# A hybrid decoder trunk on eight cores, rebuilt: transposed layouts, sample columns in the prompt blocks, chunk-dense state-space matmuls, stored tables and a list-scheduled instruction order

## The chip, the cores and the metric

The kernel runs on all eight cores of one Trainium2 chip, as two dies of four cores (0 to 3 and 4 to 7). Each core has its own prompt of 2048 positions and 16 of the 128 sample rows; the cores exchange nothing. The metric is the device time of the slowest core in microseconds (us). Rearranging arrays on the host, before and after the launch, is not in it.

A program on all eight cores has a second, slower state in some executions, in which the cores of one die, or of both, show a lower granted TensorE clock: in a run of the kernel before that took 5631.45 us, cores 4 to 7 took 5607 to 5630 us at a mean clock of 0.796 to 0.800, and cores 0 to 3 took 5072 to 5088 us at 0.908 to 0.919. Only executions in the fast state are compared here. Engine names are those of the profile: PE is the matmul engine, DVE is VectorE, ACT is ScalarE, POOL is GpSimd, SP is SyncE. A name such as L643 is a line of the kernel in question, so the same code can have another number in another version.

## The reference, cut to what matters

Four layers work on x of width 1024. A layer has a short convolution branch and a diagonal complex state-space branch, which are gated and merged, and then a feed-forward block. The same trunk runs over the prompt without a starting state, and over the sample rows, one position each, with a given state.

```python
def _layer(x, conv_buf, h0_re, h0_im, ...):
    h = _rmsnorm(x, norm1_g)
    z = h @ w_in                       # 1024 -> 4096: zb, zc, zv, zu, ga, gs
    conv_out, new_buf = _conv_causal(zc * zv, conv_buf, conv_w, conv_b)   # width 3
    ya = zb * conv_out
    ys, hr, hi = _s5(zu, h0_re, h0_im, lam_re, lam_im, log_dt, b_re, b_im, c_re, c_im, d_skip)
    gy = jax.nn.gelu(ys, approximate=False)
    ys = gy * jax.nn.sigmoid(gy @ w_glu + b_glu)
    m = jax.nn.sigmoid(ga) * (ya @ w_branch[:512]) + jax.nn.sigmoid(gs) * (ys @ w_branch[512:])
    x = x + m @ w_out
    h2 = _rmsnorm(x, norm2_g)
    gate, up = jnp.split(h2 @ w_gate_up, [2816], axis=-1)
    return x + (jax.nn.silu(gate) * up) @ w_down, new_buf, hr, hi

def _s5(u, ...):      # 32 groups of 16 channels, each with 64 complex states
    # state_t = abar * state_{t-1} + bbar u_t ;  y_t = Re(c . state_t) + d * u_t
```

## The kernel before: the parts that matter

Prompt positions go through in two halves of 1024, all four layers for one half and then for the other. Half 0 also carries the 16 sample rows, as a block of its own:

```python
def blocks(half):
    bl = [(0, 512, "p"), (512, 512, "p")]
    if half == 0:
        bl.append((1024, NS, "s"))          # NS = 16 columns
    return bl
```

The state-space recurrence is cut into chunks of T = 8 positions. Within a chunk everything is a matmul against tables (WBF, KF, CAF) that are powers of the state matrix times B and C. Between chunks VectorE rotates, scans, and rotates back. The matmuls use tiles of 32 rows or columns of the array and strided reads of the activations:

```python
for j in range(T):                      # part_a: within the chunk
    for tau in range(j + 1):
        for rg in range(4):
            mm(PSUM[b][32*rg:32*rg+32, j:512:T], KF[buf][:, tau, 32*rg:32*rg+32],
               R[32 rows..., UT + f, c0 + j - tau:c0 + 512:T], ...)      # 64 columns each
...
for j in range(T):                      # part_d: from the incoming state
    for rg in range(4):
        for ri in range(2):
            mm(PSUM[b][32*rg:32*rg+32, j:512:T], CAF[buf][:, ri, j+1, rg, :],
               HBF[:, ri, 4*f+rg, kb:kb+64], ...)
...
if f + 2 < 4:
    ssm_prep_ck(l, f + 2, f % 2)        # tables of quarter f + 2, built in line by VectorE
```

The tables of a layer are built for half 0 and again for half 1. The order of instructions on each engine is the order in which the program emits them. Weights come straight from their arrays with a casting DMA, 256 columns by 1024 rows a unit, into a ring of slots.

Of the kernel before, what the change touches and what calls it, by code (L numbers as in the profile page):

```python
# [12 lines left out]
D = 1024  # L13
# [5 lines left out]
T = 8  # L19
# [3 lines left out]
DBG = {"layers": DEPTH, "phases": None, "halves": 2}  # L23

class Op:
    __slots__ = ("eng", "fn", "deps", "needed", "val", "sem")

class Sched:
    ENGS = ("pe", "act", "dve", "pool", "sp")

    def __init__(self):
        self.prog = {e: [] for e in self.ENGS}
        self.last_w = {}
        self.readers = {}
        self.last_dma = {}

    def op(self, eng, fn, reads=(), writes=(), deps=(), dma_sem=None, mode=None):
        d = list(deps)
        forced = None
        if eng == "pe" and dma_sem is None:  # L40
            lp = getattr(self, "last_pe", None)
            if lp is not None and mode != self.last_pe_mode:
                forced = lp
        for k in reads:
            w = self.last_w.get(k)
            if w is not None:
                d.append(w)
        for k in writes:
            w = self.last_w.get(k)
            if w is not None:  # L50
                d.append(w)
            d.extend(self.readers.get(k, {}).values())
        if dma_sem is not None and dma_sem in self.last_dma:
            d.append(self.last_dma[dma_sem])
        o = Op()
        o.eng = eng
        o.fn = fn
        o.needed = False
        o.val = None
        o.sem = dma_sem  # L60
        dd = []
        seen = set()
        for x in d:
            if id(x) in seen:
                continue
            seen.add(id(x))
            if x.sem is None and x.eng == "pe" and eng == "pe" and dma_sem is None:
                continue
            x.needed = True
            dd.append(x)  # L70
        if forced is not None and id(forced) not in seen:
            forced.needed = True
            dd.append(forced)
        o.deps = dd
        if eng == "pe" and dma_sem is None:
            self.last_pe = o
            self.last_pe_mode = mode
        if dma_sem is not None:
            o.needed = True
            self.last_dma[dma_sem] = o  # L80
        rk = dma_sem if dma_sem is not None else eng
        for k in reads:
            self.readers.setdefault(k, {})[rk] = o
        for k in writes:
            self.last_w[k] = o
            self.readers[k] = {}
        self.prog[eng].append(o)
        return o

    def finalize(self):  # L90
        cnt = {e: 0 for e in self.ENGS}
        dcnt = {}
        for e in self.ENGS:
            for o in self.prog[e]:
                if o.sem is not None:
                    dcnt[o.sem] = dcnt.get(o.sem, 0) + 16
                    o.val = dcnt[o.sem]
                elif o.needed:
                    cnt[e] += 1
                    o.val = cnt[e]  # L100

    def runner(self, e, sems, dsems):
        def body(eng):
            waited = {}
            for o in self.prog[e]:
                for x in o.deps:
                    if x.sem is not None:
                        key = ("d", x.sem)
                        sh = dsems[x.sem]
                    else:  # L110
                        key = ("e", x.eng)
                        sh = sems[x.eng]
                    if waited.get(key, 0) >= x.val:
                        continue
                    waited[key] = x.val
                    eng.wait_ge(sh, x.val)
                ins = o.fn(eng)
                if o.sem is not None:
                    ins.then_inc(dsems[o.sem], 16)
                elif o.needed:  # L120
                    ins.then_inc(sems[e], 1)
        return body

def build():
# [8 lines left out]
    xp = din("xp", [SEQ, D])  # L133
    xs = din("xs", [NS, D])
    sconv_in = din("sconv", [DEPTH, NS, 2, CW])
    sre_in = din("sre", [DEPTH, NS, 2048])
    sim_in = din("sim", [DEPTH, NS, 2048])
    norm1_g = din("norm1_g", [DEPTH, D])
    w_in = din("w_in", [DEPTH, D, 4096])
    conv_w = din("conv_w", [DEPTH, 3, CW])  # L140
    conv_b = din("conv_b", [DEPTH, CW])
    lam_re = din("ssm_lam_re", [DEPTH, 32, 64])
    lam_im = din("ssm_lam_im", [DEPTH, 32, 64])
    log_dt = din("ssm_log_dt", [DEPTH, 32])
    b_re = din("ssm_b_re", [DEPTH, 32, 64, 16])
    b_im = din("ssm_b_im", [DEPTH, 32, 64, 16])
    c_re = din("ssm_c_re", [DEPTH, 32, 16, 64])
    c_im = din("ssm_c_im", [DEPTH, 32, 16, 64])
    ssm_d = din("ssm_d", [DEPTH, CW])
    w_glu = din("w_glu", [DEPTH, CW, CW])  # L150
    b_glu = din("b_glu", [DEPTH, CW])
    w_branch = din("w_branch", [DEPTH, D, D])
    w_out = din("w_out", [DEPTH, D, D])
    norm2_g = din("norm2_g", [DEPTH, D])
    w_gate_up = din("w_gate_up", [DEPTH, D, 2 * DFF])
    w_down = din("w_down", [DEPTH, DFF, D])
    final_g = din("final_g", [1, D])

    yp = dout("yp", [SEQ, D])
    ysm = dout("ysm", [NS, D])  # L160
    pconv_o = dout("pconv", [DEPTH, 2, CW])
    pre_o = dout("pre", [DEPTH, 16, 128])
    pim_o = dout("pim", [DEPTH, 16, 128])
    sconv_o = dout("sconv_o", [DEPTH, NS, 2, CW])
    sre_o = dout("sre_o", [DEPTH, NS, 2048])
    sim_o = dout("sim_o", [DEPTH, NS, 2048])
# [6 lines left out]
    NSLOT = 5  # L173
# [3 lines left out]
    RING = sb("RING", [128, NSLOT, 2048], BF16)  # L177
    NSCR = 8
    SCR = sb("SCR", [128, NSCR, 512])
    NSCB = 5  # L180
    SCB = sb("SCB", [128, NSCB, 512], BF16)
    GS = sb("GS", [128, 2, 16, 128])
    HBF = sb("HBF", [128, 2, 16, 129], BF16)
    TW = sb("TW", [128, 2, 16, 128])
    R8T = sb("R8T", [128, 16])
    TP = sb("TP", [128, 160])
    HC = sb("HC", [128, DEPTH, 2, 16])
    CONVST = sb("CONVST", [128, DEPTH, 2, 4])
    PT = sb("PT", [128, 256])
    LAMT = sb("LAMT", [128, 2, 64])  # L190
    LDT = sb("LDT", [128, 64])
# [3 lines left out]
    MASK2 = sb("MASK2", [128, 2])  # L195
    MASK4 = sb("MASK4", [128, 4])
    MASKC = sb("MASKC", [128, 128])
    MV = sb("MV", [128, 9, 16])
    PWR = sb("PWR", [128, 2, 9, 16])
    BXF = sb("BXF", [128, 2, 16, 32])  # L200
    BXB = sb("BXB", [128, 2, 16, 32], BF16)
    CXF = sb("CXF", [128, 2, 4, 128])
    WBF = [sb(f"WBF{i}", [128, 8, 2, 128], BF16) for i in range(2)]
    CAF = [sb(f"CAF{i}", [128, 2, 9, 4, 32], BF16) for i in range(2)]
    KF = [sb(f"KF{i}", [128, 8, 128], BF16) for i in range(2)]
    SST = sb("SST", [128, 2, 16, NS])
    SSTB = sb("SSTB", [128, 2, 16, NS], BF16)
    SNEW = sb("SNEW", [128, 2, 16, NS])
    SCV = sb("SCV", [128, 2, 4, NS])
    CINS = sb("CINS", [128, 4, NS])  # L210
    PSUM = [es.enter_context(nc.psum_tensor(f"ps{i}", [128, 512], F32)) for i in range(8)]
    NLD = 4
    sems = {e: es.enter_context(nc.semaphore(f"s_{e}")) for e in Sched.ENGS}
    dsem_names = [f"w{i}" for i in range(NSLOT)] + [f"ld{i}" for i in range(NLD)] + [f"st{i}" for i in range(4)]
    dsems = {k: es.enter_context(nc.semaphore(f"d_{k}")) for k in dsem_names}

    S = Sched()
    PHN = {"p": "init"}
    st = {"bank": 0, "scr": 0, "scb": 0, "ld": 0, "st": 0}

    def bank():
        b = st["bank"]
        st["bank"] = (b + 1) % 8
        return b

    def scr(n=1):
        if st.get("ffn"):
            if st.get("in_pf"):
                i = st.get("scr_pf", 0)
                if i + n > 6:  # L230
                    i = 0
                st["scr_pf"] = (i + n) % 6
                return i
            assert n == 1
            i = st.get("scr_ffn", 6)
            st["scr_ffn"] = 13 - i
            return i
        i = st["scr"]
        if i + n > NSCR:
            i = 0  # L240
        st["scr"] = (i + n) % NSCR
        return i

    def scb():
        i = st["scb"]
        st["scb"] = (i + 1) % NSCB
        return i

    def ldsem():
        i = st["ld"]  # L250
        st["ld"] = (i + 1) % NLD
        return f"ld{i}"
# [1079 lines left out]
```

## Time and profile before

The kernel's recorded runs were 5085.59, 5161.33, 5350.16 and 5457.22 us; the fast state is the low end of these. The profiled execution was fast: 5078.3 us, all cores between 5063 and 5078 us.

| reading | value | view |
|---|---|---|
| PE busy | 4300.6 us, 85% | first part of the page |
| DVE busy | 2603.9 us, 51% | first part of the page |
| 512-column matmuls in a dense stretch | 280 in 60.0 us, 214 ns each | windows |
| full-array matmuls of 512 columns (projections and norms) | 9728 + 5120 + 288 | groups by shape |
| matmuls altogether | 38,212 | first part of the page |

First the page of the kernel before: the span, the busy times, the weights' DMA queue and the chain that ended last.

```profile
span 5078.3 us, 99036 instructions; the slowest of 8 cores (5063.4 to 5078.3 us)
...
PE 4300.6 (85%) x38212; PEld 2288.2 (45%) x38212; DVE 2603.9 (51%) x4750; ACT 1031.0 (20%) x1985; POOL 434.5 (9%) x526
...
q0 software_dynamic: 479104, 243.30, 37.8%
...
PE 73%; DVE 15%; issue 6%; DMA 4%; ACT 3%; DVEq 0%; ACTq 0%; POOL 0%; SPq 0%; POOLq 0%
```

The engine that bounds the kernel is PE, but a quarter of the chain is something else. The windows view shows where. Its columns are the stretch in us, its length, the busy time (and number of instructions) of PE, weight load, DVE, ACT and POOL, the granted clock, the DMA share and GB/s. The first line is a state-space stage of half 1, the second a feed-forward stretch.

```profile
4620.00:4680.00 60.00, 25.78 (x905) 23.59 (x909) 40.41 (x59) 4.50 (x6) 0.00 (x0) 0.70 0.01 2
4920.00:4980.00 60.00, 60.00 (x280) 27.20 (x278) 13.43 (x20) 7.16 (x12) 7.95 (x10) 1.00 0.67 84
```

In the dense stretch, 280 matmuls fill the 60 us exactly, at a granted clock of 1.00. In the state-space stage, 905 tiny matmuls keep PE busy for 26 us, and the mean granted clock is 0.70; by the waits of this window PE waits 20 us for VectorE and 17 us for ScalarE. The view of waits names what PE waits for in such stages: CAF is a table, HBF the incoming state.

```profile
PE ps L760 <- DVE CAF L746: 140.1, 18, 10.3
PE ps L288 <- ACT HBF L993: 129.7, 16, 11.6
```

The sample rows cost separate matmuls. This is the timeline of PE (start, length, what, how many).

```profile
486.20 0.55 PE L288 MATMUL ps<-H,RING 128*128 128x16 bf16 x16
486.61 0.35 PE L288 MATMUL ps<-R,RING 128*128 128x16 bf16 x8
486.81 0.38 PE L288 MATMUL ps<-H,RING 128*128 128x512 bf16 x1
```

Twenty-four matmuls of 16 columns take 0.61 us, 25 ns each. There are 3712 of them in projections.

One yardstick is used throughout. Give every matmul in the trace its time in a dense stretch (214 ns for 512 columns, in proportion for others, not under 25 ns; 0.6 of that, the author's estimate, for the tiles of 64 rows). The sum is the PE work of the kernel; what a stretch of time lasts beyond the work in it is its loss. For the kernel before, the work is 4028 us and the loss 1050 us. The yardstick is an estimate worked out from the trace, not a record: a recount strictly in proportion gives 4005 us of work here and 3369 us (where 3380 is used below) for the changed kernel, less than 1% lower, and no reading turns on the difference.

### The profile page before, as it was taken

What the parts mean: (1) busy time and instruction counts of PE and PEld (TensorE: products, weight loads), DVE (VectorE), ACT (ScalarE), POOL (GpSimd) and SP (SyncE); (2) the same over time, 40 slices, a digit from 0 to 9 for tenths busy, and PEclk for the clock granted to TensorE, in tenths of its full rate; (3) what the DMA queues carried; (4) which work ended last, traced back from release to release, by engine and by line L of the source; (5) the groups of instructions that cost most, each with busy time, mean ns of one, the idle gap of its engine ahead of it and who ended that gap; (6) DMA issues with size and microseconds to landing.
All of it is one profiled execution on the core that took longest, in us unless ns stands there. A gap on an engine that the chain in (4) does not pass through costs nothing.

```text
span 5078.3 us, 99036 instructions; the slowest of 8 cores (5063.4 to 5078.3 us)
## 1 busy us (share of the span) xinstructions
PE 4300.6 (85%) x38212; PEld 2288.2 (45%) x38212; DVE 2603.9 (51%) x4750; ACT 1031.0 (20%) x1985; POOL 434.5 (9%) x526
## 2 busy tenths in 40 slices
PE   1577999778997789986999869996999879996999
PEld 1344444544445444454444544444444444444444
DVE  2664373643736536365473564647455654646423
ACT  0202212122121121212312212131221212121211
POOL 0000011000110001100111001110111001110110
PEclk8688999888998889988999889998999889988999
DMA  2123454224452244521555326542455326541564
GB/s 31 43 29 41 58 67 63 29 30 62 65 66 34 31 60 59 71 37 18 69 67 75 77 31 76 73 58 27 63 73 71 43 31 81 68 52 25 67 75 76
DMA packets 536699, 275.69 MB, mean 54 GB/s; under 512 B 60170, under 2 KB 531666, under 8 KB 535986
## 3 DMA queue, kind: packets, MB, share of 16 engines
q0 software_dynamic: 479104, 243.30, 37.8%
q1 hardware_dynamic: 57138, 26.07, 2.0%
q8 instruction: 315, 5.16, 0.4%
q14 instruction: 142, 1.16, 0.1%
HBM read 502.88 MB, written 9.85 MB: 101 GB/s over the span
## 4 chain that ended last, share of the span: by engine, by line
PE 73%; DVE 15%; issue 6%; DMA 4%; ACT 3%; DVEq 0%; ACTq 0%; POOL 0%; SPq 0%; POOLq 0%
PE ps L288 68%; DVE SCR L298 6%; DVE GS L987 2%; DMA RING<-w_branch 2%; DVE GS L298 2%; PE ps L711 1%; DVE H L469 1%; PE ps L787 1%; PE ps L962 1%; PE ps L1262 1%; ACT SCB L460 1%; DVE CAF L298 1%; PE ps L1241 1%; ACT SCR L464 0%; DVE SCR L1027 0%
## 5 line engine op out<-in xcount | busy, mean ns | idle before, releaser
L288 PE MATMUL ps<-H,RING 128*128 128x512 bf16 (+1 forms) x12160 | 2270.6, 343 | 71.3 <-DVE SCR L298 35.0
L288 PEld LDWEIGHTS ps<-H,RING 128*128 128x128 bf16 x12160 | 1029.2, 99 | 1282.9 <-issue 189.6
L288 PE MATMUL ps<-R,RING 128*128 128x512 bf16 (+1 forms) x6400 | 1193.7, 341 | 51.7 <-DMA RING<-w_branch 43.8
L288 PEld LDWEIGHTS ps<-R,RING 128*128 128x128 bf16 x6400 | 537.2, 98 | 674.6 <-issue 92.9
L298 DVE TENSOR_TENSOR R<-SCR,ps 128x512 bf16<-128x512 f32 x520 | 300.5, 583 | 705.1 <-PE ps L288 648.3
L298 DVE TENSOR_TENSOR X<-X,ps 128x512 f32<-128x512 f32 (+1 forms) x480 | 272.4, 581 | 415.8 <-PE ps L288 415.5
L1189 ACT ACTIVATE SCR<-ps 128x512 f32<-128x512 f32 (+1 forms) x440 | 226.0, 514 | 1204.3 <-PE ps L288 1051.0
L298 DVE TENSOR_TENSOR SCR<-SCR,ps 128x512 f32<-128x512 f32 x320 | 183.8, 582 | 452.7 <-PE ps L288 452.7
L288 PE MATMUL ps<-R,KF 128*32 128x64 bf16 (+1 forms) x9280 | 278.8, 296 | 48.5 <-DVE KF L770 32.2
L288 PEld LDWEIGHTS ps<-R,KF 128*32 128x32 bf16 x9280 | 267.8, 118 | 65.2 <-issue 64.9
L411 POOL DMA_DIRECT2D RING<-w_in x128 | 112.8, 884 | 1949.8 <-PE ps L288 1948.2
L460 ACT ACTIVATE SCB<-X 128x512 bf16<-128x512 f32 (+1 forms) x360 | 172.5, 536 | 504.5 <-DVE X L298 244.4
L411 POOL DMA_DIRECT2D RING<-w_gate_up x176 | 154.0, 877 | 1275.1 <-PE ps L288 1261.1
L469 DVE SCALAR_TENSOR_TENSOR H<-X,PT,SCR 128x512 bf16<-128x512 f32 (+1 forms) x320 | 181.8, 642 | 89.8 <-ACT SCR L466 82.7
L288 PE MATMUL ps<-HBF,CAF 128*32 128x64 bf16 x4096 | 92.0, 291 | 140.1 <-ACT HBF L993 129.7
L288 PE MATMUL ps<-SCB,ONESB 128*128 128x512 bf16 (+1 forms) x360 | 125.4, 412 | 85.6 <-ACT SCB L460 79.7
L298 DVE TENSOR_TENSOR SCR<-PWR,CXF 128x1152 f32<-128x1152 f32 x128 | 173.7, 1357 | 18.5 <-DMA sconv_o<-SCR 7.5
L1143 ACT ACTIVATE SCR<-ps 128x512 f32<-128x512 f32 x160 | 82.3, 514 | 440.3 <-PE ps L288 436.4
L411 POOL DMA_DIRECT2D RING<-w_down x128 | 103.2, 808 | 706.2 <-PE ps L288 705.5
L298 DVE TENSOR_TENSOR SCR<-TW,GS 128x512 f32<-128x512 f32 x256 | 159.6, 685 | 3.3
L298 DVE TENSOR_TENSOR SCR<-PWR,BXF 128x1024 f32<-128x1024 f32 x128 | 156.5, 1222 | 9.1 <-DVE SCR L298 0.5
L288 PEld LDWEIGHTS ps<-HBF,CAF 128*32 128x32 bf16 x4096 | 84.0, 147 | 145.9 <-issue 145.8
(141 smaller groups left out, 2652.0 us busy)
## 6 DMA issues: line engine op xcount, KB each, us to landing
RING<-w_gate_up POOLq DMA_DIRECT2D x176, 512.0 KB, 6.4
RING<-w_in POOLq DMA_DIRECT2D x128, 512.0 KB, 7.9
RING<-w_down POOLq DMA_DIRECT2D x64, 512.0 KB, 7.7
RING<-w_branch POOLq DMA_DIRECT2D x32, 512.0 KB, 6.7
RING<-w_out POOLq DMA_DIRECT2D x32, 512.0 KB, 8.2
SCR<-xp SPq DMA_DIRECT2D x16, 512.0 KB, 5.0
RING<-w_down POOLq DMA_DIRECT2D x32, 256.0 KB, 4.3
yp<-SCR SPq DMA_DIRECT2D x16, 512.0 KB
```

The source lines that it names most:

```text
L288: return S.op("pe", lambda e: e.matmul(out, lhsT=lhsT, rhs=rhs, start=start, stop=stop, **kw).annotate(ph_), reads=reads, writes=writes, m ...
L298: return S.op(eng, lambda e: e.tensor_tensor(out=out, in0=a, in1=b, op=op), reads=reads, writes=writes)
L411: S.op("pool", lambda e, ap=ap, kt=kt, ncols=ncols, slot=slot: e.dma_start(out=RING[:, slot, 0:kt * ncols].rearrange("p (k c) -> p k c", k ...
L460: act(lambda e, kt=kt, j=j, c0=c0, n=n: e.activation(out=SCB[:, j, 0:n], in_=X[:, kt, c0:c0 + n], func=AF.Square), [bkey("X", kt, c0)], [( ...
L469: dve(lambda e, kt=kt, i=i, c0=c0, n=n: e.scalar_tensor_tensor(out=H[:, kt, c0:c0 + n], in0=X[:, kt, c0:c0 + n], scalar=pcol(gname, gidx0 ...
L711: S.op("pe", lambda e, b=b, src=src, mm_=mm_, rg=rg: e.matmul(PSUM[b][32 * rg:32 * rg + 32, mm_ * 128:(mm_ + 1) * 128], lhsT=src[:, mm_, r ...
L787: S.op("pe", lambda e, b=b, q=q, qq=qq, raw=raw: e.matmul(PSUM[b][:, qq * NS:(qq + 1) * NS], lhsT=raw[0:NS, q * 128:(q + 1) * 128], rhs=ID ...
L962: S.op("pe", lambda e, b=b, q=q, qq=qq, ri=ri: e.matmul(PSUM[b][0:NS, qq * 128:(qq + 1) * 128], lhsT=SNEW[:, ri, q, :], rhs=IDF[:], start= ...
L987: dve(lambda e, ri=ri, q=q: e.tensor_tensor_scan(out=GS[:, ri, q, :], data0=bc(R8T[:, q:q + 1], [[0, 128]]), data1=GS[:, ri, q, :], initia ...
L1143: act(lambda e, bga=bga, ia=ia, n=n: e.activation(out=SCR[:, ia, 0:n], in_=PSUM[bga][:, 0:n], func=AF.Sigmoid), [("ps", bga)], sk(ia))
L1189: act(lambda e, bg=bg, i=i, n=n: e.activation(out=SCR[:, i, 0:n], in_=PSUM[bg][:, 0:n], func=AF.Silu), [("ps", bg)], sk(i))
L1241: S.op("pe", lambda e, b=b, kk=kk, kt=kt, stg=stg, nr=nr: e.matmul(PSUM[b][:, kk * 128:kk * 128 + nr], lhsT=stg[0:nr, kt * 128:(kt + 1) * ...
```

## The change

The intent is to give PE fewer and larger matmuls, and to keep it fed.

1. Activations and outputs are transposed on the host, so PE transposes of x and y go. The weights are packed on the host into units of 128 long rows.
2. The 16 sample columns ride in the blocks of half 0: 384, 384 and 272 columns instead of 512, 512 and 16.
3. The activations are stored so that a chunk's position and channel together fill the 128 rows of the array. A state-space quarter then needs 16 matmuls into the chunk states, 8 within the chunk and 32 from the incoming state, of 128 columns each, instead of hundreds of narrow ones. To turn channel-major into chunk-major rows, the input and the output go through DRAM and back (`du`, `dy`).
4. The tables of a layer are built once, during half 0, written to DRAM (`stash`), and loaded again for each use.
5. All operations go into a list with a duration each. A planner then fixes the order on each engine: at each step the ready operation with the lowest priority number that can have its buffers. Pools hand out the buffers during this planning.

```diff
+BLKS = [[Blk(0, 0, 384, (0, 1, 2)), Blk(1, 384, 384, (3, 4, 5)), Blk(2, 768, 272, (6, 7, 8))], ...
+    wpk = din("wpk", [DEPTH, NU, 128, 2048])
+    S.dma("pool", lambda e: e.dma_start(out=t[:, 0:n], in_=wpk[l, ui, :, 0:n]), (), [(t,)], 128 * n * 2)
...
+    PP = Pool("psum", 8, lambda s: PSUM[s], reserve=3)
+    SP_ = Pool("sc", NSC, lambda s: SC[:, s, :], reserve=4)      # NSC = 9 scratch slots
+    RBP = Pool("rb", 2, lambda s: RBT[:, s, :], reserve=-1)
+    VP = Pool("v", 1, lambda s: VT[:, s, :], reserve=-1)
...
+        def feasible(o, t):              # may operation o start now? (it needs a slot for each new tile)
+            ...
+                if len(free) < len(tls):
+                    return False
+                fr = p.tiles[p.front] if p.front < len(p.tiles) else None
+                if fr not in tls:
+                    if p.reserve < 0 or len(free) - len(tls) < p.reserve:
+                        return False
...
+        def prep_f(f):                   # tables of one quarter
+            bn, z1, z2 = SP_.new(), SP_.new(), SP_.new()
+            ...                          # 12 operations of 512 columns on VectorE
+            y1, y2 = SP_.new(), SP_.new()
+            di1, di2 = SP_.new(), SP_.new()
+            x1_ = SP_.new()
+            S.dma("sp", ... out=stash[l, f], in_=tab[:, 0:2560] ...)
...
+        def ssm_f(f):                    # one state-space quarter
+            # PE: 16 matmuls into gr, gi   (+ 16 of 16 columns for the samples)
+            # VectorE: 6 operations of rotation, 8 scans, 4 operations into vt
+            # PE: 8 matmuls within the chunk into yb, 32 from vt into yb;  ACT: gelu;  DMA: dy, back
...
+        if half == 0 and l + 1 < DEPTH:
+            prep(l + 1, S.shift + 250)   # emitted at the start of the feed-forward of layer l
```

The rule in `feasible`: The tile that was emitted first and has no slot yet (the front of its pool) may take any free slot. Everything emitted later may take one only if `reserve` slots stay free after it. A negative reserve means strict order. The rule keeps the plan from locking up.

## The prediction

> **What bounds it now.** TensorE. The page gives PE 85% busy, the chain of waits 73% PE, 15% DVE, 6% issue, 4% DMA. The profile is of the fast state (5078 us; I take 5350 and 5457 us as slow). By shape (groups of instructions) the 14,848 matmuls of 128x512 are the work. In dense stretches of the windows view 280 of them take 60.0 us, 214 ns each, at granted clock 1.00 on all eight cores: 3182 us. [...]
>
> The other 1900 us: sample-only matmuls with 16 columns (3712 of them, 24 take about 0.6 us on the timeline: 93 us); the state-space stage, about 190 to 240 us per layer, where windows show PE 26 to 45 us of 60 at a clock of 0.70 to 0.86 and DVE 40 to 50 us (17,000 tiny matmuls, tables built in line; PE waits 140 us for CAF, 130 us for HBF); tables rebuilt in half 1; and a start of about 360 us with PE busy 176. Half-0 layers take about 648 us, half-1 layers 557 us, against 398 us of dense matmul.
>
> **What the change does.** Same dense columns. Sample columns ride in blocks of 384/384/272, so the 93 us become about 25. At 214, 161 and 114 ns (estimates scaled from 214) projections and norms cost about 3270 us. The 17,000 tiny matmuls become about 2400 of 128 columns or less plus their table work: about 130 us. PE sum about 3400 us at full clock. DVE falls from 2604 to about 1990 us (687 ns per 512-column op, 484 per scan): about 58% of the new span; tables are built once (half 0, under the FFN) and reloaded. Weights arrive in long rows instead of about 508-byte packets (243 MB in 479,104); six slots instead of five: DMA is not the bound. The list scheduler fills the SSM's serial DVE part (about 11 us per quarter, 43 us per layer) with conv and gate projections (about 75 us of PE), so most of it is hidden.
>
> **What remains exposed.** Start: x load, then serial table building on DVE (about 100 us) with little PE work: 100 us. About 10 us of PE waits per layer for the state-space round trips through DRAM: 80 us. Change of half (new x only after the old is normed): 25 us. End: 15 us. [...]model error of the static order, clock drops: 100 us. Sum 3400 + 320, about 3720 us.
>
> **Predicted: 3740 us, 8 in 10 within 3560 to 4120.** Faster by over 2%: 0.98; within 2%: 0.01; slower: 0.01.
>
> **Right if:** PE about 93% busy; mean clock above 0.95; windows of every later layer 420 to 450 us; 512-column matmuls still 214 ns apart; DVE about 2000 us; the chain over 85% PE; waits of PE on DVE/ACT/DMA together under 250 us outside the first layer.
>
> **Wrong if:** [...]the static order puts a late instruction at the head of a queue (long PE waits for PSUM or the DRAM round trips); the table building delays the first layers by more than 150 us; weight loads land late (PE waiting on RING).

The losses 100, 80, 25, 15 and 100 come to 320 us, and with 3400 us of work to 3720 us.

## The result, and the profile after

The changed kernel took 4043.53 us in the median of 4 runs (4037.78 to 4053.94), with correct outputs. The ratio to the kernel before is 0.795, with a 95% interval of 0.793 to 0.797. Ratios are the mean time of one kernel's fast runs over that of the other's in the same rounds, so they are not quite the ratio of the medians quoted here.

The page of the changed kernel:

```profile
span 4042.0 us, 63569 instructions; the slowest of 8 cores (4025.0 to 4042.0 us)
...
PE 3568.7 (88%) x21736; PEld 1993.4 (49%) x21736; DVE 1879.5 (46%) x3694; ACT 981.6 (24%) x1910; POOL 345.5 (9%) x546
...
q0 software_dynamic: 67968, 243.30, 36.1%
q1 hardware_dynamic: 118768, 120.08, 9.7%
...
PE 80%; DVE 10%; issue 5%; DMA 3%; ACT 2%; DVEq 0%; SPq 0%; ACTq 0%
```

The same 243.30 MB of weights come in a seventh of the packets, and the new traffic through DRAM is there (q1 moves 120 MB, where it moved 26 MB), but the DMA share of the chain is 3%. PE has 21,736 matmuls instead of 38,212. The chain has 80% PE, not the 85% and more that was forecast.

In the yardstick above, the work of the changed kernel is 3380 us and its loss 662 us. So 648 us of the gain of 1036 us came from less work on PE (4028 to 3380), and 388 us from less loss (1050 to 662); the strict recount gives 635 and 401. The prediction had 3400 us of work and 320 us of loss. The windows view tells where the loss lies.

```profile
360.00:420.00 60.00, 24.84 (x169) 15.12 (x170) 54.71 (x124) 9.83 (x18) 9.40 (x9) 0.65 0.24 63
540.00:600.00 60.00, 60.00 (x410) 39.84 (x408) 13.06 (x26) 3.74 (x8) 4.22 (x8) 1.00 0.52 79
660.00:720.00 60.00, 28.82 (x374) 21.04 (x372) 31.28 (x65) 9.97 (x29) 1.06 (x2) 0.63 0.45 116
900.00:960.00 60.00, 22.50 (x152) 13.62 (x152) 54.64 (x123) 8.67 (x15) 10.84 (x10) 0.68 0.22 62
2700.00:2760.00 60.00, 48.66 (x350) 24.41 (x349) 43.74 (x84) 16.29 (x34) 2.63 (x5) 0.83 0.63 159
3000.00:3060.00 60.00, 60.00 (x280) 27.18 (x278) 11.69 (x17) 2.39 (x4) 4.22 (x8) 1.00 0.44 82
```

The second and the last line are feed-forward stretches as they should be: PE full, clock 1.00, and in half 1 the same 280 matmuls in 60 us as before. The first and fourth line are also feed-forward stretches of half 0, at the place where the tables of the next layer are built. There PE did 25 and 22 us of work in 60, and VectorE was busy nearly all the time. The third and fifth are state-space stages, of half 0 and half 1.

Adding up the windows, with the forecast beside them (its 80 us for eight state-space stages are split by layers):

| where | forecast loss, us | loss after, us |
|---|---|---|
| start, 0 to 240 us | 100 | 151 |
| tables built in the feed-forward of layers 0, 1 and 2 of half 0 (300 to 480, 900 to 1020, 1440 to 1560 us) | 0 ("under the FFN") | 163 |
| state-space stages of half 0, layers 1 to 3 | 30 (10 a layer) | 154 |
| state-space stages of half 1, and of layer 0 of half 0 (which is in the start) | 50 | 93 |
| change of half | 25 | 47 |
| end | 15 | 16 |
| everything else | 100 | 38 |
| sum | 320 | 662 |

The view of waits tells what PE waits for:

```profile
PE ps L1032 <- DVE VT L999: 75.7, 21, 5.1
PE ps L874 <- DVE SC L545: 65.7, 18, 7.5
PE ps L874 <- DVE TB L545: 60.1, 7, 16.0
...
PE ps L1010 <- DVE SC L985: 37.6, 11, 3.5
PE ps L885 <- DVE TAB L867: 33.2, 10, 4.1
PE ps L967 <- DMA UU<-du: 19.5, 4, 8.2
```

L874 and L885 are the matmuls of the table building; L967, L1010 and L1032 are those of the state-space quarters. Columns: us in total, times, longest us. Three groups (L874 twice, L885), 159 us together, belong to the table building; the other three to the state-space quarters, 133 us.

Why does PE stand still in a feed-forward stretch? The timeline of VectorE in the changed kernel, in the stretch of the fourth window line:

```profile
911.30 0.69 DVE L545 TENSOR_TENSOR SC<-TB 128x512 f32<-128x512 f32 x1
911.91 0.18 DVE L545 TENSOR_TENSOR TB<-TB 128x16 f32<-128x16 f32 x1
912.09 0.69 DVE L545 TENSOR_TENSOR SC<-SC 128x512 bf16<-128x512 f32 x1
912.70 0.18 DVE L545 TENSOR_TENSOR TB<-TB 128x16 f32<-128x16 f32 x1
```

L545 is the helper that the table building uses. From 900.4 to 928.1 us VectorE runs nothing but table operations: no multiplication of the feed-forward (L1186) is among them. PE stands still until it can run the matmuls of the table building (L874, L885), and its next projection (L643) starts only at 921.09 us:

```profile
912.93 0.58 PE L874 MATMUL ps<-IDB,SC 128*128 128x128 bf16 x4 [16.02 <-DVE TB L545]
921.09 6.35 PE L643 MATMUL ps<-H,RING 128*128 128x384 bf16 x32
```

Two readings are possible. Either VectorE has no room and its table work displaces the feed-forward, or the feed-forward is not ready to run, because the planner would not give it buffers. The first is what the VectorE column of the windows suggests.

### The profile page after: what moved, and what is told of

The parts are those of the page before. It is cut to its first block, busy times and chain, and to the rows that moved or that the text cites. A ratio compares the mean times of both kernels' runs of the same rounds, so it can differ in the third digit from the quotient of the medians.

```text
span 4042.0 us, 63569 instructions; the slowest of 8 cores (4025.0 to 4042.0 us)
## 1 busy us (share of the span) xinstructions
PE 3568.7 (88%) x21736; PEld 1993.4 (49%) x21736; DVE 1879.5 (46%) x3694; ACT 981.6 (24%) x1910; POOL 345.5 (9%) x546
## 3 DMA queue, kind: packets, MB, share of 16 engines
q0 software_dynamic: 67968, 243.30, 36.1%
## 4 chain that ended last, share of the span: by engine, by line
PE 80%; DVE 10%; issue 5%; DMA 3%; ACT 2%; DVEq 0%; SPq 0%; ACTq 0%
PE ps L643 76%; DVE H L695 2%; DVE SC L545 2%; PE ps L1032 1%; DVE RBT L993 1%; DVE TB L545 1%; PE ps L674 1%; DMA X<-xT 1%; DMA UU<-du 1%; PE ps L967 1%; DVE SC L981 0%; DVE TAB L545 0%; DMA yT<-SC 0%; DVE SC L983 0%; DVE SC L982 0%
## 5 line engine op out<-in xcount | busy, mean ns | idle before, releaser
L643 PE MATMUL ps<-H,RING 128*128 128x512 bf16 (+2 forms) x12160 | 2259.7, 344 | 44.9 <-DVE X L1165 15.4
L643 PEld LDWEIGHTS ps<-H,RING 128*128 128x128 bf16 x12160 | 1205.6, 99 | 1029.4 <-issue 123.7
L643 PE MATMUL ps<-R,RING 128*128 128x384 bf16 (+2 forms) x6400 | 1197.5, 338 | 1.3 <-DVE R L1145 1.2
L643 PEld LDWEIGHTS ps<-R,RING 128*128 128x128 bf16 x6400 | 626.2, 98 | 496.3 <-issue 4.7
L1186 DVE TENSOR_TENSOR R<-SC,ps 128x384 bf16<-128x384 f32 (+2 forms) x440 | 255.9, 583 | 866.9 <-PE ps L643 866.7
L1185 ACT ACTIVATE SC<-ps 128x384 f32<-128x384 f32 (+2 forms) x440 | 225.7, 515 | 1405.8 <-PE ps L643 1369.3
L631 POOL DMA_DIRECT2D RING<-wpk x472 | 250.5, 532 | 3384.4 <-PE ps L643 2961.8
L1165 DVE TENSOR_TENSOR X<-X,ps 128x384 f32<-128x384 f32 (+2 forms) x480 | 276.3, 583 | 518.7 <-PE ps L643 512.2
L672 ACT ACTIVATE SCB<-X 128x384 bf16<-128x384 f32 (+2 forms) x360 | 189.7, 543 | 306.9 <-PE ps L674 173.4
L695 DVE SCALAR_TENSOR_TENSOR H<-X,PRM,SC 128x384 bf16<-128x384 f32 (+2 forms) x320 | 189.7, 667 | 64.5 <-ACT SC L679 64.2
L1131 ACT ACTIVATE SC<-ps 128x384 f32<-128x384 f32 (+1 forms) x160 | 81.6, 515 | 233.6 <-PE ps L643 210.5
L1032 PE MATMUL ps<-VT,TAB 64*128 64x128 bf16 x1024 | 60.6, 270 | 78.0 <-DVE VT L999 75.7
L1156 ACT ACTIVATE SC<-ps 128x384 f32<-128x384 f32 (+1 forms) x160 | 80.7, 515 | 198.7 <-PE ps L643 153.4
L874 PE MATMUL ps<-IDB,SC 128*128 128x128 bf16 x128 | 16.1, 267 | 126.0 <-DVE SC L545 65.7
L545 DVE TENSOR_TENSOR SC<-TB 128x512 f32<-128x512 f32 x128 | 97.6, 795 | 0.1
```

Of the source, the lines that this page charges most:

```text
L545: fn = lambda e: e.tensor_tensor(out=out(), in0=a(), in1=b(), op=op)
L631: S.dma("pool", lambda e: e.dma_start(out=t[:, 0:n], in_=wpk[l, ui, :, 0:n]), (), [(t,)], 128 * n * 2)
L643: subs.append((lambda e, u=u, kw=kw, c=c, src=src, i=i: e.matmul(ps[:, 0:blk.n], lhsT=u.ap(kw, c), rhs=src(blk), start=(i == 0), stop=(i = ...
L672: act(lambda e, kt=kt, q=q: e.activation(out=q[:, 0:n], in_=X[:, kt, blk.c0:blk.c0 + n], func=AF.Square), xkeys(kt, blk), [(q,)], n)
L695: dve(lambda e, kt=kt, xi=xi, g=g: e.scalar_tensor_tensor(out=H[:, kt, blk.c0:blk.c0 + n], in0=xi(), scalar=g, in1=rs[:, 0:n], op0=ALU.mul ...
L1032: subs.append((lambda e, q=q, g2=g2, i=i, ri=ri, yb=yb, CDv=CDv, vv=vv: e.matmul(yb[g2][:, q * 128:(q + 1) * 128], lhsT=CDv()[64 * g2:64 * ...
```

## The experiments

Ten kernels were run. All edits are against the changed kernel. Eight give correct outputs; two give wrong ones.

**1. No tables for layers 1 to 3** (e1_no_tables). How much does the building of tables cost in all? Layers 1 to 3 use the tables of layer 0, and their own are not built. The outputs are wrong.

```diff
-            prep(l + 1, S.shift + 250)
+            pass
-   ... in_=stash[l, f] ...  R8[:, l, ...]  E128[:, l, ri]  EA[:, l, ri]
+   ... in_=stash[0, f] ...  R8[:, 0, ...]  E128[:, 0, ri]  EA[:, 0, ri]
```

> The tables of layers 1 to 3 are not built (layer 0's are reused everywhere: wrong result on purpose), all else as in the changed kernel. It prices the table building in the three feed-forward stretches, where the windows of the changed kernel lose about 170 us of TensorE. If table building is what stalls the feed-forward there (slots or VectorE, not told apart here): 3800 to 3880 us against 4040, and no feed-forward window of half 0 loses more than 5 us. If those stretches are slow for another reason (late weights, the clock, wrong durations in the planner): over 3980 us.

It took 3807.68 and 3808.29 us: 236 us less. The windows of the stretches in question:

```profile
360.00:420.00 60.00, 60.00 (x408) 39.77 (x407) 12.93 (x25) 11.88 (x26) 4.24 (x8) 1.00 0.55 81
900.00:960.00 60.00, 60.00 (x411) 39.92 (x409) 12.82 (x25) 1.78 (x4) 4.23 (x8) 1.00 0.45 79
```

The feed-forward stretches are full. Their 163 us are gone, and the state-space stages of half 0 and the start lost less too. So the building of tables costs about 236 us in place of the 0 that was forecast; some 11 us of this are its own matmuls, by the yardstick. Which resource it costs is not yet told.

**2. The scratch moved** (e2_scratch). For one quarter, table building takes 8 scratch tiles from the pool of 9 slots (bn, z1, z2, y1, y2, di1, di2, x1_). The state-space buffers RBT and VT are idle in a feed-forward stretch. Here z1, z2, y1 and y2 use RBT, and di1 and di2 use VT; bn and x1_ stay in the pool. VectorE does exactly the same operations. If VectorE is full, nothing changes.

```diff
-            bn, z1, z2 = SP_.new(), SP_.new(), SP_.new()
+            bn, zp, yp_, dp = SP_.new(), RBP.new(), RBP.new(), VP.new()
+            z1, z2, y1, y2 = (zp, 0), (zp, 512), (yp_, 0), (yp_, 512)
-            y1, y2 = SP_.new(), SP_.new()
-            di1, di2 = SP_.new(), SP_.new()
+            di1, di2 = (dp, 0), (dp, 512)
```

> The same table building, the same instructions on every engine; only its scratch tiles move from the pool SC (up to 8 of its 9 slots, while the feed-forward may take a slot only if 4 more stay free) to buffers of the state-space stage that are idle then. Slot theory: the feed-forward is no longer refused slots, the stretches of 40 us lost per layer mostly vanish, 3880 to 3960 us. VectorE theory (the builder's own 100 us of VectorE per layer are the cost, VectorE was 54.7 of 60 us busy): same VectorE work, 4000 to 4060 us.

It took 3918.06 us in the median of 4 runs (3915.82 to 3923.74), correct: 125 us less with the same VectorE work (1867.7 us busy against 1879.5). The same windows:

```profile
360.00:420.00 60.00, 12.32 (x96) 7.37 (x96) 57.78 (x98) 8.58 (x16) 16.50 (x12) 0.53 0.19 76
900.00:960.00 60.00, 57.82 (x441) 38.55 (x439) 56.27 (x119) 14.60 (x31) 8.87 (x13) 1.00 0.58 110
```

In the second line VectorE is busier than before (56.27 against 54.64 us), and yet PE does 57.82 us of work, where it had done 22.50. VectorE had room for both. Its timeline now shows the feed-forward (here L1188) between the table operations, and PE runs 160 matmuls of projections on end where it had stood still:

```profile
911.16 0.68 DVE L545 TENSOR_TENSOR TAB<-RBT 128x512 bf16<-128x512 f32 x1
911.76 0.18 DVE L545 TENSOR_TENSOR EE<-TB 128x16 f32<-128x16 f32 x1
...
913.26 0.55 DVE L1188 TENSOR_TENSOR R<-SC,ps 128x384 bf16<-128x384 f32 x1
913.73 0.19 DVE L545 TENSOR_TENSOR TB<-EE 128x32 f32<-128x32 f32 x1
```

```profile
899.74 23.55 PE L643 MATMUL ps<-H,RING 128*128 128x272 bf16 x160
```

So the reading "VectorE is full" falls, and "the feed-forward got no scratch slots" stands, for layers 1 and 2. By the windows these two stretches lost 105 us before and lose 8 us now. The stretch of layer 0 (first line) is worse than before, 12.32 against 24.84 us of PE; that is taken up in experiments 7 to 10.

**3. In emission order** (e3_in_order). What is the planner's order worth? PE, ACT and VectorE take their operations as emitted; SyncE and GpSimd, which issue the DMAs, stay list-scheduled.

```diff
-LISTSCHED = True
+LISTSCHED = False
-            if LISTSCHED:
+            if LISTSCHED or e in ("sp", "pool"):
```

> List scheduling off for TensorE, ScalarE and VectorE: each engine keeps the order in which the program emits the operations (DMA queues stay list-scheduled). Prices the list scheduling by itself. If it hides the state-space stage behind projections as the prediction says: 250 to 350 us slower than the changed kernel, 4290 to 4400 us, still far under the kernel before. If the gain comes from shapes and layouts alone: under 4100 us.

It took 4390.65 and 4380.57 us, some 340 us more, with correct outputs. With the work on PE unchanged, the loss is then about 1010 us, near the 1050 us of the kernel before. So less work on PE made about 650 us of the gain, and the order the rest: nearly all of what was gained in loss came from interleaving stages.

**4. Calibrated durations** (e4_calibrated). The planner's durations are a model. If the plan were good and the chip merely slower than the model, correcting the model would help. The fixed costs were set from the trace.

```diff
-TT_ = lambda n: 0.155 + n * 1.04e-3
+TT_ = lambda n: 0.07 + n * 1.04e-3
-ACT_ = lambda n: 0.17 + n * 0.833e-3
+ACT_ = lambda n: 0.07 + n * 0.833e-3
-                r = o.end + self.LAT - s.offs[i]
+                r = o.end + self.LAT + (0.16 if o.eng == "dve" else 0.12 if o.eng == "act" else 0.0) - s.offs[i]
```

> Only the durations by which the planner orders are changed, to those that the trace shows: VectorE operations of 512 columns start 0.60 us apart when independent[...]. If PE stands before the tables' transposes because the planner thought the tables would be ready sooner: at least 80 us faster, under 3960 us. If the loss is in what the slots allow, not in wrong durations: 4000 to 4080 us.

In the changed kernel most operations of 16 columns on VectorE that follow one another start 0.28 us apart, and two operations of 512 columns on ScalarE start 0.52 us apart (2687.41 and 2687.93 us).

It took 4035.89 and 4033.48 us, 9 us less. A mismatch in these durations is not the cause (those of PE and of the DMAs were not changed). The idle stretches stand in the plan itself: the planner, run again on the host, gives a plan of 4110 us for the changed kernel and of 4111 us with the corrected durations. So they come from what the planner is allowed to do.

**5. No round trips** (e5_no_trips). The state-space input and output wait for a write to DRAM and a read back. Here each layer reads what the layer before wrote (two DRAM buffers in turn), so the data are there long before. The outputs are wrong.

```diff
+        wp = l % 2
+        rp = 1 - wp if (l or not hs) else wp
-   ... out=du[f, ...]   in_=du[f, ...]   out=dy[f, ...]   in_=dy[f, ...]
+   ... out=du[wp, f, ...]  in_=du[rp, f, ...]  out=dy[wp, f, ...]  in_=dy[rp, f, ...]
```

> The state-space stage reads the input and output that the layer before left in DRAM (two buffers by layer parity; wrong result on purpose): the same transfers, but nothing waits for a round trip of its own layer. If the round trips are what the stage exposes: the losses of about 25 us per layer in half 1 fall below 10 us and the time is 3900 to 3960 us. If the trips are hidden as predicted at 10 us per layer or less and the stage is held by VectorE or slots: over 3980 us.

The profiled run took 4006.77 us, but two cores held it up. The view of cores:

```profile
core 2: 4001.7 us, clock 0.927
core 3: 4005.2 us, clock 0.928
core 4: 3944.9 us, clock 0.944
```

Cores 2 and 3 had a granted clock of 0.81 for 388 and 391 us, cores 6 and 7 for 73 and 80 us, and cores 0, 1, 4 and 5 for none. The other two runs were slow, and their times are left out; their undisturbed die, cores 4 to 7, took 3938 to 3947 us. By its own time the profiled run falls in the range that was written for the rival (over 3980 us), so the reading rests on the cores without a drop of the clock. Cores 0, 1, 4 and 5 took 3944 to 3947 us, where they took 4025 to 4039 us with the trips (means 3945 and 4035). So the round trips cost about 90 us in all. In half 1 their removal takes the loss of a state-space stage from about 23 us to about 6. The same window of half 1 as above, on the slowest core, shows it: PE 55.25 us, clock 1.00, where it was 48.66 us and 0.83.

```profile
2700.00:2760.00 60.00, 55.25 (x414) 26.97 (x412) 48.66 (x87) 27.88 (x51) 4.23 (x8) 1.00 0.80 184
```

**6. The rotation doubled** (e6_double_rotation). Is the serial VectorE part of a quarter hidden, as forecast? Three of the six operations of the rotation are issued twice, with the same results: 96 operations in all, which at the 0.60 us between their starts is 58 us.

```diff
             dve(... out=t2, in0=SIN(), in1=gi ...)
+            dve(... out=t2, in0=SIN(), in1=gi ...)
             dve(... out=t3, in0=COS(), in1=gi ...)
+            dve(... out=t3, in0=COS(), in1=gi ...)
             dve(... out=t4, in0=SIN(), in1=gr ...)
+            dve(... out=t4, in0=SIN(), in1=gr ...)
```

> Three of the six rotation operations on VectorE are issued twice in each of 32 state-space quarters (idempotent, correct result): 96 more operations, 0.60 us apart in the trace, 58 us. If the serial VectorE chain of the stage is on the critical path: 45 to 65 us slower, 4085 to 4105 us. If projections hide it (my prediction): under 20 us slower.

It took 4107.07 and 4106.55 us as fast runs (ratio 0.808, 0.806 to 0.811): 63 us more for 58 us of added operations. In the profiled run cores 0 to 3 had a granted clock of 0.81 for 62 to 73 us; cores 4 to 7, which had none of it, took 59 us more than in the changed kernel (means 4093 and 4034). Nothing of it was hidden. The timeline of PE shows a quarter of layer 1, half 0, in the changed kernel first:

```profile
681.26 0.26 PE L971 MATMUL ps<-UU,TAB 128*64 128x16 bf16 x2
684.97 1.01 PE L1010 MATMUL ps<-UU,TAB 128*128 128x128 bf16 x8 [3.45 <-DVE SC L985]
689.17 2.31 PE L1032 MATMUL ps<-VT,TAB 64*128 64x128 bf16 x32 [3.19 <-DVE VT L999]
```

and in the kernel with the doubled rotation:

```profile
685.16 0.26 PE L971 MATMUL ps<-UU,TAB 128*64 128x16 bf16 x2
691.04 1.01 PE L1013 MATMUL ps<-UU,TAB 128*128 128x128 bf16 x8 [5.62 <-DVE SC L988]
694.87 2.31 PE L1035 MATMUL ps<-VT,TAB 64*128 64x128 bf16 x32 [2.82 <-DVE VT L1002]
```

From the last matmuls into the chunk states to the first of the last group it is 7.9 us (681.26 to 689.17), and 9.7 us with the three added operations (685.16 to 694.87). Between them PE has the quarter's own 8 matmuls and no projection. In half 0 the stage runs at the pace of its VectorE chain. In half 1 the chain is exposed only together with the trips: experiment 5 left the chain as it is, and the loss fell to about 6 us a stage.

**7. The combined version** (e7_combined). Three edits: the moved scratch, a reserve of 2 instead of 4 on the scratch pool, and the matmuls within the chunk held until the first product from the incoming state is there, so that they do not take two banks of PSUM early.

```diff
+ (the edits of experiment 2)
-    SP_ = Pool("sc", NSC, lambda s: SC[:, s, :], reserve=4)
+    SP_ = Pool("sc", NSC, lambda s: SC[:, s, :], reserve=2)
-                        skip_group_check=True), [(tab,), (ut_,)], MMN(128)))
+                        skip_group_check=True), [(tab,), (ut_,), (vt, 0)], MMN(128)))
```

> The scratch move of e2_scratch, SC slots kept in reserve 2 instead of 4, and the feed-through matmul of the state-space output bound to the first rotated scan result, so that its two PSUM banks are held later and shorter. Slot theory: fewer refusals also outside table building; 3810 to 3880 us, the fastest of all correct kernels. If slots do not matter: as e2_scratch within 20 us.

It took 3809.29 us in the median of 4 runs (3807.66 to 3811.26), correct: ratio 0.7496 (0.7479 to 0.7513) to the kernel before, and 5.8% less than the changed kernel by the medians (3809.29 and 4043.53). It beats both, and lies 0.7 us under the range that was written for it. Its page:

```profile
PE 3517.9 (92%) x21736; PEld 1967.6 (52%) x21736; DVE 1855.0 (49%) x3694; ACT 997.3 (26%) x1922; POOL 327.9 (9%) x546
...
PE 84%; DVE 7%; issue 4%; DMA 3%; ACT 2%; DVEq 0%; SPq 0%; ACTq 0%
```

**8 to 10. The combined version taken apart.** Which of its edits made the 109 us beyond the moved scratch? Three more runs, on one chip.

Experiment 8 (e8_scratch_res2) has the scratch and the reserve:

```diff
+ (the edits of experiment 2)
-    ... reserve=4)
+    ... reserve=2)
```

> The moved scratch of the table building, and the reserve on the scratch pool lowered from 4 to 2, without the third edit of the combined version (the intra-chunk product held until the incoming state is computed). Theory: after the table building has left the pool, the reserve of 4 of 9 slots is what still delays the state-space stages of half 0, because later work may take a scratch slot only while 4 stay free; the reserve then carries nearly all of the 109 us that the combined version gained over the moved scratch alone. Then 3810 to 3840 us. Rival: the third edit, which keeps a bank of PSUM from being taken early, carries the larger part; then 3880 to 3910 us.

Experiment 9 (e9_scratch_late) has the scratch and the held matmuls:

```diff
+ (the edits of experiment 2)
-                        skip_group_check=True), [(tab,), (ut_,)], MMN(128)))
+                        skip_group_check=True), [(tab,), (ut_,), (vt, 0)], MMN(128)))
```

> The moved scratch and the held intra-chunk product, with the reserve on the scratch pool left at 4. It is the other half of the split. If the reserve is what binds, 3900 to 3920 us (as the moved scratch alone, 3918). If the PSUM bank is what binds, 3820 to 3850 us.

Experiment 10 (e10_res2_alone) has the reserve alone:

```diff
-    ... reserve=4)
+    ... reserve=2)
```

> The changed kernel with only the reserve lowered from 4 to 2; the table building keeps its 8 of 9 scratch slots. If the loss under the half-0 feed-forward comes from the slots that the table building holds, lowering the reserve helps there little (one or two slots more at best) and the time stays above 3960 us; if the reserve alone were the cause, it would fall to about 3810 to 3850 us without moving anything.

| edits | median of 4, us | ratio to before | against the changed kernel |
|---|---|---|---|
| none (the changed kernel) | 4043.53 | 0.795 | 0 |
| reserve (10) | 4074.33 | 0.801 | +31 |
| scratch (2) | 3918.06 | no interval (see below) | −125 |
| scratch, held matmuls (9) | 3897.11 | 0.766 | −146 |
| scratch, reserve (8) | 3848.88 | 0.756 | −195 |
| all three (7) | 3809.29 | 0.750 | −234 |

Beside experiments 1 to 4 all but one of the runs of the kernel before were slow, so no ratio is given for them; the four runs of experiment 2 agree within 8 us. On top of the scratch the reserve carries 69 us and the held matmuls 21 us; together they give 109, so each is worth some 20 us more beside the other. Experiment 8 landed just above the range that was written for the reserve, so "nearly all" was too much: it is about two thirds. Experiment 9 landed just below the range of 3900 to 3920 us that was written for the reserve. The held matmuls act where they were meant to: with the scratch and the reserve already moved, they take the state-space stages of half 0 from some 42 to some 35 us a layer. The smaller reserve (experiment 8) acted in another place than was expected. The state-space stages of half 0 still lose some 42 us a layer with it, much as with the moved scratch alone (37 to 45). What it repaired is the one stretch that the moved scratch had left, in the feed-forward of layer 0; here the window of experiment 8, to be held against the 12.32 us of PE in experiment 2:

```profile
360.00:420.00 60.00, 57.82 (x443) 38.59 (x441) 57.19 (x110) 14.61 (x32) 15.42 (x17) 1.00 0.57 115
```

With the reserve alone (experiment 10), PE gets even less done in these stretches than in the changed kernel, 13.04 and 15.50 us against 24.84 and 22.50:

```profile
360.00:420.00 60.00, 13.04 (x106) 8.33 (x107) 53.80 (x117) 7.50 (x12) 13.94 (x7) 0.56 0.11 44
900.00:960.00 60.00, 15.50 (x110) 9.48 (x108) 52.44 (x130) 9.77 (x19) 5.05 (x5) 0.60 0.21 45
```

The slots that the tables hold are thus the cause, and a smaller reserve is no substitute for them. Why layer 0's stretch needs both edits, and why the reserve alone makes it worse, the profile cannot tell, since it does not record which tile holds which slot. The planner can. It is plain Python in each run's kernel, and it was run again on the host with a note of every refusal. For the changed kernel and for experiments 2, 8 and 10 the replayed order puts all 440 multiplications of the feed-forward at exactly the places in VectorE's order that the trace shows. It tells three things.

- How scratch stops PE: ScalarE's activation of the feed-forward (L1185) is refused a scratch slot, so five of the eight banks of PSUM stay full of finished projections, and PE's next projection is refused a bank.
- Who holds the slots: not only the tiles of the quarter in work. Each layer's table building has two more scratch tiles for the states of the samples, which are loaded by DMAs that wait for nothing, and GpSimd fills di tiles of later quarters ahead. Such early takers can fill the pool down to the reserve.
- The two open cases: in experiment 2, in the stretch of layer 0, the sample states of layers 1 to 3 hold five of the nine slots; four are free, and a reserve of 4 refuses every activation. In layer 1 they hold three. A reserve of 2 is then enough (experiment 8). With the reserve alone (experiment 10) the early takers, with di tiles among them as in the changed kernel, go on to seven of nine, and the two slots left are again the reserve.

## Why the prediction was right or wrong

**The direction was right, and the result, 4043.5 us, lies within the range of 3560 to 4120 us. The central figure of 3740 us was 304 us too low.** That the result lies within the range is owed to the width of the range: the loss was 662 us where 320 us were forecast.

*PE sum about 3400 us at full clock*: right. It is 3380 us. The terms of it hold as well: the 512-column matmuls stay 214 ns apart (280 in 60.00 us in half 1), and blocks of 384, 384 and 272 columns take the sample rows along (410 matmuls in 60.00 us of half 0, 146 ns each, which is the mean of 161, 161 and 114).

*DVE about 2000 us*: right within 7%, 1880 us. *DMA is not the bound*: right, 3% of the chain. *"At full clock"* held for the dense stretches in the fast state: the granted clock was 1.00 there, and 0.81 for 76 us on two cores only. It could have gone otherwise: all four runs of the changed kernel were fast, but two of three of experiment 5 were not.

*"tables are built once (half 0, under the FFN) and reloaded"*: this is the first step that failed. The forecast gave the table building no time. It cost 163 us in the feed-forward stretches by the windows, and 236 us in all by experiment 1. The forecast put VectorE at about 58% of the span, which leaves room under the feed-forward. That was true of VectorE (46%) and beside the point: experiment 2 kept every VectorE operation and recovered 125 us by freeing scratch slots. The work that was to be hidden held the buffers of the work that was to hide it, and stood before it in the queue for them. The code said so: eight scratch tiles a quarter, a pool of nine, and a reserve of 4; in the replayed plan table building holds all nine at times. The prediction read the cost in time of each operation and did not count buffers.

*"Most of it is hidden", and "about 10 us of PE waits per layer for the state-space round trips: 80 us"*: this is the second step that failed. The stages cost about 247 us (154 and 93) without the first layer's. The forecast had named the round trips, and these cost about 90 us (experiment 5), close to its 80. What it had taken as hidden was the serial VectorE chain, 43 us a layer. Experiment 6 shows it in the open: 58 us more of it cost 63 us. In half 0 a quarter waits for its chain with no projection between (timeline under experiment 6). The replayed plan says why for layers 1 and 2: it is the same pool. Tiles of sample states and di tiles hold five slots, ScalarE's copy of a convolution projection (L1085) is refused one, and again five banks of PSUM stay full. This is part of the loss only, since experiment 1, which has none of these tiles, still loses some 35 us a stage there. In half 1, where no tables are built, the loss was the trips (experiment 5). These costs overlap with that of the tables, so they are not added: experiment 1 also took some 47 us off the state-space stages of half 0, from 154 to 107.

*Start 100, change of half 25, end 15*: the first two were too small by about 51 and 22 us (151 and 47); the end was right (16). *Model error of the static order, clock drops: 100* was too large; what is left over is 38 us. Part of what it was meant for, the drops of the clock, sits in the stages named above: in their windows the mean granted clock was 0.63 to 0.83.

*Right if: PE about 93% busy, mean clock above 0.95, later layers 420 to 450 us, chain over 85% PE, waits on other engines under 250 us*: PE was 88% busy, the clock 0.93, the chain 80% PE; the layers of half 0 took 534 to 550 us (from the first state-space matmul of one to that of the next), and PE waited 334 us for other engines and DMAs after the first 300 us. These signs fail together, as they should with 340 us more of idle time. The layers of half 1, 447 us each, met theirs. The combined version comes near them: PE 92%, clock 0.964 to 0.970, chain 84%.

*Wrong if: the static order puts a late instruction at the head of a queue (long PE waits for PSUM or the DRAM round trips)*: this came closest, but it names PSUM and DRAM; in the plan PE is indeed refused PSUM, and the buffer that bound behind it was the scratch. *The table building delays the first layers by more than 150 us*: it did delay them by about that much, though not as a delay of the start: by stealing slots under each of three feed-forward blocks.

What stays open: the loss of about 428 us in the combined version (3808 less 3380). By its windows, about 130 us lie in the start, about 35 us in each state-space stage of half 0, some 60 us around the change of half (with the first stage of half 1), and about 20 us in each later stage of half 1. Nothing was tried on the start.

## What to carry to other kernels

Work on a half-idle engine is free only if the buffers that it holds are free as well (in experiment 2 they were worth 125 us): before calling anything hidden, count the slots that it takes from every pool that it shares with the work above it, and see who comes first for them. When a busy engine is next to a stalled one, do not infer that the busy one is full; move one resource at a time and keep the operations (experiment 2 did so in some twenty lines). For a serial chain, double it and see: if the time grows by the whole of what was added, it is on the critical path, whatever the average busy share says.

## What the traces show of the chip

- The granted clock. In the fast state these runs had 1.00 in nearly all dense stretches on all eight cores (1.00 on each from 4920 to 4980 us of the kernel before, and from 540 to 600 and 3000 to 3060 us of the changed kernel). The kernel before never showed 0.81 in its profiled run. Where 0.81 was seen, it was at times on a pair of cores only: on cores 2 and 3 for 76 us in the changed kernel, and for 388 and 391 us in experiment 5, while cores 0 and 1 of the same die had none of it. In experiments 3 and 6 it was on all four cores of one die, for 59 to 126 and 62 to 73 us (mean clocks there 0.908 to 0.912, against 0.913 to 0.916 on the other die, and 0.919 to 0.920, against 0.922 to 0.925). This holds for the fast state alone. In slow executions, of which no trace is kept, a whole die has a lower mean clock (0.803 to 0.804 on cores 0 to 3 against 0.942 to 0.945 on the others in the first run of experiment 5). Why the clock was lower was not shown. A clock of 0.5 was granted for 542 to 564 us of the changed kernel's run, where PE was busy for 88% of the span, and for 231 to 279 us of the combined version's, where it was busy for 92%.
- The distance between VectorE operations. In the changed kernel, operations of 512 columns from SBUF, which record 0.68 to 0.69 us, start 0.60 to 0.61 us apart; the state-space rotations with one operand in PSUM start 0.60 us apart (681.63, 682.24, 682.83 us), too. Small operations that wait for each other take longer than one of them records: 14 operations of 16 columns on one tile in the table building take 4.11 us from 901.90 us, 0.29 us each, where a single one records 0.18 us. (After one whose result the next does not use, the next starts 0.08 us later, at 911.22 and 911.30 us.) The table building is made of such operations in good part.
- VectorE beside GpSimd. A table operation of 512 columns that records 0.68 to 0.69 us elsewhere recorded 1.54 us in experiment 2 while POOL built the next diagonal in 2.44 us. Whether the one slowed the other was not tested, and what it adds up to in this kernel was not measured. The two timelines, VectorE and then POOL:

```profile
375.27 1.54 DVE L545 TENSOR_TENSOR TAB<-RBT 128x512 bf16<-128x512 f32 x1
```

```profile
373.83 2.44 POOL L898 TENSOR_TENSOR VT<-IDF,PRM 128x512 f32<-128x512 f32 x2
```
